# Retention and cross-attention trunk on one core: folded weights stored as hi/lo pairs, four VectorE steps given to ScalarE

## The chip, the cores and the metric

The kernel runs on one core of a Trainium2 chip. The metric is the device time of one execution in microseconds, from the runs of this one core; three runs of the kernel before took 2501.79, 2500.89 and 2510.75 us, with a median of 2501.79 us. One more execution was recorded by the hardware profiler. The core has five engines with an instruction queue each: TensorE (PE in the profile; PEld is its weight load), VectorE (DVE), ScalarE (ACT), GpSimd (POOL) and SyncE (SP), which here only issues DMAs. ACT and POOL issue some DMAs too, in line with their other instructions.

## The reference, cut to what matters

One layer of a decoder trunk over 2048 tokens of width 1024, in fp32:

```python
h = rmsnorm(x, mix_norm_g)
q, k, v, g, u = split(h @ w_in)                       # four retention heads of 128, and 512 pooling channels
y_ret  = silu(g) * head_rmsnorm(retention(rope(q), rope(k) * 128**-0.5, v), ret_gn_g)
y_pool = pool_mixer(u, pool_w, pool_scale)            # windowed means, one 128x128 matrix per group
x = x + concat([y_ret, y_pool]) @ w_out
# cross-attention into 256 memory tokens, four heads of 256
q = rmsnorm(x, xa_norm_g) @ xa_wq;  k, v = split(rmsnorm(mem, mem_norm_g) @ xa_wkv)
x = x + softmax(q @ k.T / 16) @ v @ xa_wo
x = x + conv_glu_ffn(rmsnorm(x, ffn_norm_g), ...)     # d_ff 2816, causal depthwise conv of width 3
return rmsnorm(x, final_norm_g)

def rope(t):      # t1, t2: the two halves of a head
    return concat([t1 * cos - t2 * sin, t2 * cos + t1 * sin])
```

## The kernel before, in words

Everything is held transposed, channels on the 128 partitions and tokens along the row. Matrix products keep fp32 accuracy with operands split in two: `split` (L230) lets ScalarE round a tile to the high part (`hi`, type fp32r) and VectorE subtract it from the source (`lo`), and `passes` (L239) multiplies hi by hi, hi by lo and lo by hi, three matmuls (L241, L242, L243) into one PSUM tile. Such a hi/lo couple is called a pair.

The tokens are worked in two blocks b = 0 and 1 of 1024 (`T`), each in two halves s of 512 (`SUB`). For a block come in order: values, four heads (gate, q and k, one `unit` each), four pooling groups, the output projection w_out (eight units n), the cross-attention (16 chunks of 128 tokens by two heads) and its output product (eight units with the weights VWd). Behind both blocks stands the FFN, done with sums of tiles in seven products in place of eight (`run`, L1324); the sums of its weights (`weight_sums`, L903) are made earlier by DMAs that SP and POOL issue between the units.

`folded_weights` (L360) does the products of weights alone, between the heads of block 0: the memory's keys with xa_wq into Md (L473), its values with xa_wo into VWd (L491), the pooling matrices with w_out into WPd (L512). A result is evacuated from PSUM by ScalarE into a tile of the arena `TT` (ten slots, called T in the profile), and `keep` (L431) sends it to DRAM from ScalarE's DMA queue as one fp32 tile. When it is used, in block 0 and again in block 1, it is loaded by SP into R (five slots of 1024), and split anew: by `pairs` (L255) into Q (three slots of a pair each) for VWd and WPd, and by `load_m` (L830) for Md, whose 16 tiles a pass go into the second half of G (first head pair; only its first two into Q) and into Z (second head pair). G's second half holds the inputs of w_out (`mix`) until w_out has read them.

A `unit` (L285) is 48 matmuls: two weight halves h by two token halves s by four contraction tiles by three passes. Five PSUM banks (`mm`) serve the units, three more (`aux`) the rest. `rope_evac` (L687) rotates q and k out of PSUM: one product with cos, two of 64 partitions with the crossed halves and sin, one add, all on VectorE. `retention` (L717) works a head as two halves of four chunks, as a generator that is advanced between the quarters of later units: scores, states, values, mixed. In `values` the four chunks' outputs are scaled by a factor per token (L772), in one VectorE instruction. In `attention` (L822) each chunk takes its maximum (L871), the exponentials with their sums on ScalarE (L875), the reciprocal (L877), a scaling of both heads' halves on VectorE (L880), and later the transposes and the split of `turn` (L847).

The order on each engine is made when the program is built: the code is recorded in program order, a scheduler with a model of the times reorders it, and each engine then runs its list strictly in that order. SP's list has all its loads and the copies for the weight sums; a DMA there that waits for its slot holds up those behind it. `tc.issue_after(fetched[0].ins)` (L911) places the copies for a weight sum behind the latest load. POOL's list has the adding DMAs of the weight sums and, between them, the 16-column copies of the pooling groups (L630, L631).

Of the kernel before, what the change touches and what calls it, by code (L numbers as in the profile page):

```python
# [8 lines left out]
F32 = mybir.dt.float32  # L9
# [6 lines left out]
P = 128  # L16
# [103 lines left out]
def trunk(ctx, tc, xT, memT, pos, w_qkgu, w_v, wkv, wqT, wo, wout_r, wout_p, poolT, w_up, w_dn, vecs, consts, outT):  # L120
# [164 lines left out]
    def unit(raw, rhs, evac, order=range(4)):  # L285


        hs = pairs(raw)
# [71 lines left out]
    def folded_weights():  # L360
# [74 lines left out]
        def tiles4(d, nh, k):  # L435
            return d[4 * nh : 4 * nh + 4, :, k, :].rearrange("n p c -> p n c")
# [23 lines left out]
        for h in range(HEADS):  # L460
            dp = [row_pairs(wqT[(2 * h + dt) * P : (2 * h + dt + 1) * P, :]) for dt in range(2)]
            for k2 in range(KT // 2):
# [6 lines left out]
                t = TT.take()  # L469
                for j in range(2):  # L470
                    k = 2 * k2 + j
                    act.activation(t.f[:, j * NMEM : (j + 1) * NMEM], ps[:, j * NMEM : (j + 1) * NMEM], AF.Identity, scale=xag[:, k : k + 1])
                keep(Md[h // 2, 2 * k2 : 2 * k2 + 2, :, (h % 2) * NMEM : (h % 2 + 1) * NMEM].rearrange("k p m -> p k m"), t, 2)  # L473
# [6 lines left out]
        for h in range(HEADS):  # L480
            dp = [row_pairs(wo[(2 * h + dt) * P : (2 * h + dt + 1) * P, :]) for dt in range(2)]
            for mt in range(2):
                for nh in range(2):
# [5 lines left out]
                    t = TT.take()  # L489
                    act.activation(t.f[:, :SUB], ps, AF.Identity, scale=rn[:, mt : mt + 1])  # L490
                    keep(tiles4(VWd, nh, 2 * h + mt), t, 4)  # L491
# [12 lines left out]
        for g in range(4):  # L504
            u = row_pairs(wout_p[g])
            for nh in range(2):
                ps = mmps()
                lh = [pw.r[:, i * SUB + g * P : i * SUB + (g + 1) * P] for i in range(2)]
                passes(ps, lh, [u.r[:, i * T + nh * SUB : i * T + (nh + 1) * SUB] for i in range(2)], True, True)
                t = TT.take()  # L510
                act.activation(t.f[:, :SUB], ps, AF.Copy)
                keep(tiles4(WPd, nh, g), t, 4)  # L512
# [170 lines left out]
    def head_inputs(h, rb, cs, fill):  # L683
# [3 lines left out]
        def rope_evac(i):  # L687
            def evac(s, ps):
# [28 lines left out]
    def retention(b, h, qkg, v, out):  # L717
# [10 lines left out]
        class Half:  # L728
# [30 lines left out]
            def values(self):  # L759
# [12 lines left out]
                tt(dve, four(self.kn.f[:, :SUB]), four(y), bcast(rr, P), ALU.mult)  # L772
# [49 lines left out]
    def attention(sums, beside, pace):  # L822
# [7 lines left out]
        def load_m(hp):  # L830

            out = mw[hp]
            for kp in range(KT // 2):
                raw = new_raw()
                fetched[0] = sp.dma_start(raw.rearrange("p (k n) -> p k n", k=2), Md[hp, 2 * kp : 2 * kp + 2].rearrange("k p n -> p k n"))
                if hp == 0 and kp == 0:

                    out += [(pr[:, 0], pr[:, 1]) for pr in pairs(raw)]
                    yield
                    continue  # L840
                for i in range(2):
                    u = third[2 * hp].r[:, (2 * kp + i) * T : (2 * kp + i + 1) * T]
                    split(raw[:, i * SUB : (i + 1) * SUB], u[:, :SUB], u[:, SUB:])
# [16 lines left out]
        for i in range(2 * KT):  # L860
# [638 lines left out]
    for b in range(NB):  # L1499
# [68 lines left out]
        for n in range(KT):  # L1568
# [7 lines left out]
            unit(load_tile(VWd[n]), rhs, add_residual(b, n, xs, acc=acc[n]))  # L1576
# [150 lines left out]
```

## Time and profile before

| | |
|---|---|
| median of three runs | 2501.79 us |
| the profiled execution: its time, its span | 2506.72 us, 2504.9 us |
| PE busy | 2442.7 us, 98% of the span |
| DVE busy | 1666.9 us, 67% |
| ACT busy | 1216.1 us, 49% |
| POOL busy | 652.4 us, 26% |
| moved by DMA | 474.28 MB, mean 189 GB/s |

The span is what the profiler saw of the program on the core; the execution's own time is a little longer. Times inside the profile count from the span's start. In a view by windows each row is a stretch of time with the busy time of each engine in it and, in parentheses, the number of its instructions, then the clock that was granted to TensorE (1.00 is full), the share of time in which the DMA engines were busy, and GB/s. In a list of groups a row has the line, the engine, the operation, the tiles written and read, the shapes, the count, then busy us and mean ns of one, and behind the bar the idle time of the engine just before them with what ended it. By the trace, block 0's folded weights and heads run from about 135 to 340 us, its w_out from about 384 us, its attention from 474.6 us; block 1 follows from about 680 us, and the FFN takes the second half.

### The profile page before, as it was taken

To read this page: it belongs to the slowest core of one execution; us is meant where nothing else is said; L and a number is where in the kernel's file an instruction comes from. 1 tells how busy PE (TensorE), PEld (TensorE's weight loads), DVE (VectorE), ACT (ScalarE), POOL (GpSimd) and SP (SyncE) were. 2 spreads that over 40 slices of the span, in tenths; PEclk is the share of its full clock that TensorE was granted. 3 is DMA by queue.
4 is the path that set the end of the run, shared out by engine and by line. 5 is a ranking of instruction groups with operands and counts; after the bars stand their busy time and mean duration, and the time that the engine had idled before them with its cause. 6 is when DMAs were issued, how large, how long until landed. Compare 5 with 4: busy or idle time off the path is not lost.

```text
span 2504.9 us, 33172 instructions
## 1 busy us (share of the span) xinstructions
PE 2442.7 (98%) x11390; PEld 2037.7 (81%) x11390; DVE 1666.9 (67%) x2574; ACT 1216.1 (49%) x2163; POOL 652.4 (26%) x579
## 2 busy tenths in 40 slices
PE   6999999999999999999999999999999999999997
PEld 6888887788788888888887888878888887888885
DVE  8646566564635675574678776886677586867875
ACT  6333423343321223434654555665555576666663
POOL 1010122100121120030237352553335154222322
PEclk9999999999999999999999999999999999999998
DMA  8363888715766764366567564755556468768951
GB/s 318 89 168 110 244 191 233 234 40 181 227 152 145 159 158 149 111 221 220 167 205 270 166 203 153 236 192 165 160 160 213 136 220 287 250 185 280 346 164 68
DMA packets 257177, 474.28 MB, mean 189 GB/s; under 512 B 26864, under 2 KB 56176, under 8 KB 257008
## 3 DMA queue, kind: packets, MB, share of 16 engines
q1 hardware_dynamic: 212336, 408.18, 49.0%
q0 software_dynamic: 19584, 34.61, 8.9%
q10 hardware_dynamic: 25088, 29.37, 3.4%
q8 instruction: 89, 1.46, 0.2%
q14 instruction: 80, 0.66, 0.1%
HBM read 370.87 MB, written 170.39 MB: 216 GB/s over the span
## 4 chain that ended last, share of the span: by engine, by line
PE 78%; DMA 8%; DVE 6%; issue 3%; POOL 2%; ACT 2%; SPq 0%; POOLq 0%; ACTq 0%; DVEq 0%
PE mm L241 25%; PE mm L242 24%; PE mm L243 24%; POOL T L216 1%; DVE Z L216 1%; DMA T<-Xd 1%; DVE Z L225 1%; DVE G L216 1%; DMA T<-xT 1%; DVE Q L216 1%; DVE T L216 1%; DMA T<-Gd 1%; POOL Z L216 1%; PE aux L749 1%; DMA R<-VWd 0%
## 5 line engine op out<-in xcount | busy, mean ns | idle before, releaser
L241 PE MATMUL mm<-G,Q 128*128 128x512 f32 (+1 forms) x1888 | 728.1, 386 | 21.8 <-ACT Q L233 11.1
L243 PE MATMUL mm<-G,Q 128*128 128x512 f32 (+1 forms) x1888 | 725.9, 385 | 4.4 <-DVE Q L216 4.2
L242 PE MATMUL mm<-G,Q 128*128 128x512 f32 (+1 forms) x1888 | 725.7, 385 | 0.7 <-DVE G L216 0.7
L241 PE MATMUL mm<-G 128*128 128x512 f32 (+1 forms) x1380 | 532.1, 387 | 10.0 <-DVE Z L216 6.3
L242 PE MATMUL mm<-G 128*128 128x512 f32 (+1 forms) x1380 | 531.7, 386 | 0.0
L243 PE MATMUL mm<-G 128*128 128x512 f32 (+1 forms) x1380 | 531.1, 385 | 0.0
L241 PEld LDWEIGHTS mm<-G,Q 128*128 128x128 f32 x1888 | 357.8, 190 | 91.1 <-ACT Q L233 11.8
L243 PEld LDWEIGHTS mm<-G,Q 128*128 128x128 f32 x1888 | 357.7, 190 | 74.3 <-DVE Q L216 5.9
L242 PEld LDWEIGHTS mm<-G,Q 128*128 128x128 f32 x1888 | 358.0, 190 | 69.4 <-DVE G L216 1.6
L225 DVE SCALAR_TENSOR_TENSOR Z<-Z,vecs 128x1024 f32<-128x1024 f32 x176 | 276.3, 1572 | 153.5 <-ACT Z L1069 145.3
L241 PEld LDWEIGHTS mm<-G 128*128 128x128 f32 x1380 | 260.4, 189 | 64.5 <-DVE Z L216 8.0
L243 PEld LDWEIGHTS mm<-G 128*128 128x128 f32 x1380 | 260.2, 189 | 51.8
L242 PEld LDWEIGHTS mm<-G 128*128 128x128 f32 x1380 | 260.1, 188 | 51.5
L1006 ACT ACTIVATE G<-R 128x512 fp32r<-128x512 f32 (+1 forms) x272 | 166.5, 615 | 197.8 <-PE mm L242 178.6
L216 DVE TENSOR_TENSOR Z<-Z,mm 128x512 f32<-128x512 f32 x284 | 192.8, 679 | 78.2 <-PE mm L243 78.0
L216 DVE TENSOR_TENSOR Q<-R,Q 128x512 fp32r<-128x512 f32 x199 | 148.6, 748 | 143.4 <-ACT Q L233 138.9
L216 POOL TENSOR_TENSOR G<-R,G 128x512 fp32r<-128x512 f32 (+1 forms) x100 | 141.9, 1420 | 376.2 <-ACT G L1006 290.9
L233 ACT ACTIVATE Q<-R 128x512 fp32r<-128x512 f32 x150 | 93.8, 627 | 234.8 <-PE mm L242 187.3
L1006 ACT ACTIVATE Q<-R 128x512 fp32r<-128x512 f32 (+1 forms) x204 | 125.0, 613 | 90.9 <-PE mm L242 73.5
L216 DVE TENSOR_TENSOR G<-R,G 128x512 fp32r<-128x512 f32 (+1 forms) x168 | 131.5, 794 | 46.7 <-ACT G L233 38.0
L216 DVE TENSOR_TENSOR G<-T,G 128x512 fp32r<-128x512 f32 (+1 forms) x168 | 125.4, 758 | 53.9 <-ACT G L955 40.7
L940 ACT ACTIVATE aux<-R 128x512 f32<-128x512 f32 (+1 forms) x184 | 105.8, 576 | 95.8 <-DVE Q L216 52.9
(222 smaller groups left out, 2911.4 us busy)
## 6 DMA issues: line engine op xcount, KB each, us to landing
R<-Ud SPq DMA_DIRECT2D x176, 256.0 KB, 2.7
T<-Gd SPq DMA_DIRECT2D x168, 256.0 KB, 4.1
R<-w_up SPq DMA_DIRECT2D x132, 256.0 KB, 3.1
Gd<-Z SPq DMA_DIRECT2D x110, 256.0 KB, 2.4
Ud<-w_up SPq DMA_DIRECT2D x88, 256.0 KB, 5.9
R<-w_qkgu SPq DMA_DIRECT2D x32, 512.0 KB, 4.4
R<-Dd SPq DMA_DIRECT2D x64, 256.0 KB, 4.0
Gd<-T SPq DMA_DIRECT2D x56, 256.0 KB, 3.1
```

What stands on the lines that cost most here:

```text
L216: return eng.tensor_tensor(out=out, in0=a, in1=b, op=op)
L225: dve.scalar_tensor_tensor(out=out, in0=a, scalar=s, in1=b, op0=op0, op1=op1)
L233: act.activation(hi, src, AF.Copy)
L241: pe.matmul(ps, lh, rh, start=start, stop=False, skip_group_check=more)
L242: pe.matmul(ps, lh, rl, start=False, stop=False, skip_group_check=more)
L243: pe.matmul(ps, ll, rh, start=False, stop=stop, skip_group_check=more)
L749: pe.matmul(col(self.kv, c), col(self.kn.f, c), self.ch(v, c, h * T), start=True, stop=True)
L940: act.activation(t, x, AF.Copy)
L1006: act.activation(p2[:, 0, :w], self.raw[i].f[:, :w], AF.Copy)
```

## The change

Four things are changed, all in one edit.

1. The folded weights are stored in DRAM as pairs. `keep` now takes the PSUM tile itself and two T slots, splits it on the spot (ScalarE the hi, VectorE the lo, both out of PSUM, with the scale applied in both), and sends two DMAs from ScalarE's queue. Md, VWd and WPd are twice as large.
2. The loads bring pairs. VWd and WPd go straight into the slots of Q with `load_pair`, and Md straight into G or Z, with no split and without R. In w_out the other half of the unit's weights (`wout_r`) is still loaded to R and split.
3. Rotary's two crossed halves are copied out of PSUM by ScalarE (64 partitions each); VectorE then multiplies the whole copied tile by sin in one instruction.
4. Softmax's division is a ScalarE activation with a scale per token in place of a VectorE instruction, and the scaling of the retention's output is four ScalarE activations, one per chunk, in place of one VectorE instruction.

```diff
-    Md = drp.tile([2, KT, P, SUB], F32, tag="Md", name="Md")
-    VWd = drp.tile([KT, P, KT, P], F32, tag="VWd", name="VWd")
+    Md = drp.tile([2, KT, P, 2, SUB], F32, tag="Md", name="Md")
+    VWd = drp.tile([KT, 2, P, 2, 4, P], F32, tag="VWd", name="VWd")
...
-    WPd = drp.tile([KT, P, 4, P], F32, tag="WPd", name="WPd")
+    WPd = drp.tile([KT, P, 2, 4, P], F32, tag="WPd", name="WPd")
...
+    def load_pair(src):
+        pr = new_pair()
+        fetched[0] = sp.dma_start(pr.bitcast(F32), src)
+        return pr
...
-        hs = pairs(raw)
+        hs = raw if isinstance(raw, list) else pairs(raw)
...
-        def keep(dst, t, n):
-            act.dma_start(dst, t.f[:, :SUB].rearrange("p (n c) -> p n c", n=n))
-            t.free()
+        def keep(dsts, ps, n, g=None):
+            two = [TT.take() for _ in range(2)]
+            hi, lo = (t.f[:, :SUB].bitcast(F32R) for t in two)
+            w = SUB // n
+            for j in range(n if isinstance(g, list) else 1):
+                at = slice(j * w, (j + 1) * w) if isinstance(g, list) else slice(0, SUB)
+                split(ps[:, at], hi[:, at], lo[:, at], g[j] if isinstance(g, list) else g)
+            for t, dst in zip(two, dsts):
+                act.dma_start(dst, t.f[:, :SUB].rearrange("p (n c) -> p n c", n=n))
+                t.free()
...
-                    t = TT.take()
-                    act.activation(t.f[:, :SUB], ps, AF.Identity, scale=rn[:, mt : mt + 1])
-                    keep(tiles4(VWd, nh, 2 * h + mt), t, 4)
+                    to = VWd[4 * nh : 4 * nh + 4, h // 2, :, :, 2 * (h % 2) + mt]
+                    keep([to[:, :, i].rearrange("n p c -> p n c") for i in range(2)], ps, 4, rn[:, mt : mt + 1])
...
+                act.activation(w[0:64], ps[64:128], AF.Copy)
+                act.activation(w[64:128], ps[0:64], AF.Copy)
                 tt(dve, d, ps, c, ALU.mult)
-                tt(dve, w[0:64], ps[64:128], sn[0:64], ALU.mult)
-                tt(dve, w[64:128], ps[0:64], sn[64:128], ALU.mult)
+                tt(dve, w, w, sn, ALU.mult)
...
-                tt(dve, four(self.kn.f[:, :SUB]), four(y), bcast(rr, P), ALU.mult)
+                for c in range(4):
+                    act.activation(col(self.kn.f, c), col(y, c), AF.Identity, scale=rr[:, c : c + 1])
...
-                raw = new_raw()
-                fetched[0] = sp.dma_start(raw.rearrange("p (k n) -> p k n", k=2), Md[hp, 2 * kp : 2 * kp + 2].rearrange("k p n -> p k n"))
-                if hp == 0 and kp == 0:
-
-                    out += [(pr[:, 0], pr[:, 1]) for pr in pairs(raw)]
-                    yield
-                    continue
-                for i in range(2):
-                    u = third[2 * hp].r[:, (2 * kp + i) * T : (2 * kp + i + 1) * T]
-                    split(raw[:, i * SUB : (i + 1) * SUB], u[:, :SUB], u[:, SUB:])
+                for k in (2 * kp, 2 * kp + 1):
+                    if hp == 0 and kp == 0:
+                        pr = load_pair(Md[hp, k])
+                        out.append((pr[:, 0], pr[:, 1]))
+                        continue
+                    u = third[2 * hp].r[:, k * T : (k + 1) * T]
+                    fetched[0] = sp.dma_start(u.bitcast(F32), Md[hp, k].rearrange("p i n -> p (i n)"))
                     out.append((u[:, :SUB], u[:, SUB:]))
...
-                ts(dve, ej, ej, sm[:, j : j + 1], ALU.mult)
+                act.activation(ej, ej, AF.Identity, scale=sm[:, j : j + 1])
...
-            fetched[0] = sp.dma_start(raw[:, SUB:], WPd[n].rearrange("p k c -> p (k c)"))
+            pr = new_pair()
+            split(raw[:, :SUB], pr[:, 0], pr[:, 1])
+            raw = [pr, load_pair(WPd[n].rearrange("p i k c -> p i (k c)"))]
...
-            unit(load_tile(VWd[n]), rhs, add_residual(b, n, xs, acc=acc[n]))
+            unit([load_pair(VWd[n, h].rearrange("p i k c -> p i (k c)")) for h in range(2)], rhs, add_residual(b, n, xs, acc=acc[n]))
```

More of the change, by code (lines that the diff above doesn't have):

```diff
@@ L429, in row_pairs @@
             return u
-        def keep(dst, t, n):
-            act.dma_start(dst, t.f[:, :SUB].rearrange("p (n c) -> p n c", n=n))
-            t.free()
-        def tiles4(d, nh, k):
-            return d[4 * nh : 4 * nh + 4, :, k, :].rearrange("n p c -> p n c")
+        def keep(dsts, ps, n, g=None):
[8 more added lines that the diff above has]
+                t.free()
         kk = B.take(4)
@@ L468, in folded_weights @@
                         passes(ps[:, j * NMEM : (j + 1) * NMEM], w, (kp4[:, 2 * h + dt, 0], kp4[:, 2 * h + dt, 1]), dt == 0, dt == 1)
-                t = TT.take()
[L470 to L473, printed above, removed]
+                to = Md[h // 2, 2 * k2 : 2 * k2 + 2, :, :, (h % 2) * NMEM : (h % 2 + 1) * NMEM]
+                keep([to[:, :, i].rearrange("k p m -> p k m") for i in range(2)], ps, 2, [xag[:, 2 * k2 + j : 2 * k2 + j + 1] for j in range(2)])
             for u in dp:
@@ L488, in folded_weights @@
                         passes(ps, lh, w, dt == 0, dt == 1)
-                    t = TT.take()
-                    act.activation(t.f[:, :SUB], ps, AF.Identity, scale=rn[:, mt : mt + 1])
-                    keep(tiles4(VWd, nh, 2 * h + mt), t, 4)
+                    to = VWd[4 * nh : 4 * nh + 4, h // 2, :, :, 2 * (h % 2) + mt]
+                    keep([to[:, :, i].rearrange("n p c -> p n c") for i in range(2)], ps, 4, rn[:, mt : mt + 1])
             for u in dp:
@@ L509, in folded_weights @@
                 passes(ps, lh, [u.r[:, i * T + nh * SUB : i * T + (nh + 1) * SUB] for i in range(2)], True, True)
-                t = TT.take()
-                act.activation(t.f[:, :SUB], ps, AF.Copy)
-                keep(tiles4(WPd, nh, g), t, 4)
+                to = WPd[4 * nh : 4 * nh + 4, :, :, g]
+                keep([to[:, :, i].rearrange("n p c -> p n c") for i in range(2)], ps, 4)
             u.free()
```

## The prediction

> **What bounds the kernel now.** I began with the page's totals.
>
> ```profile
> span 2504.9 us, 33172 instructions
> PE 2442.7 (98%) x11390; PEld 2037.7 (81%) x11390; DVE 1666.9 (67%) x2574; ACT 1216.1 (49%) x2163; POOL 652.4 (26%) x579
> ```
>
> TensorE is busy 98% of the span, so 2504.9 − 2442.7 = 62 us of idle and some slow clock is all that work on other engines can give back, and only in the stages that the change touches. The windows say where it lies. In this view a row is a stretch of time, the busy us of each engine with its instructions, the clock granted to TensorE, DMA share and GB/s.
>
> ```profile
> 250.00:275.00 25.00, 24.48 (x111) 20.05 (x110) 16.65 (x36) 10.30 (x17) 2.44 (x3) 1.00 0.83 240
> 275.00:300.00 25.00, 24.67 (x132) 20.87 (x131) 9.45 (x17) 12.02 (x20) 2.44 (x3) 1.00 0.87 251
> 300.00:325.00 25.00, 25.00 (x127) 21.11 (x127) 18.02 (x48) 8.67 (x27) 4.96 (x6) 1.00 0.81 182
> 325.00:350.00 25.00, 25.00 (x135) 21.49 (x135) 15.18 (x33) 8.63 (x21) 4.25 (x8) 1.00 0.82 224
> 350.00:375.00 25.00, 24.70 (x126) 20.72 (x125) 17.48 (x46) 5.14 (x15) 7.44 (x14) 1.00 0.86 184
> 375.00:400.00 25.00, 21.24 (x91) 16.70 (x90) 15.96 (x28) 4.28 (x7) 9.12 (x14) 1.00 0.81 183
> 400.00:425.00 25.00, 25.00 (x112) 20.68 (x111) 17.42 (x29) 10.98 (x19) 4.38 (x6) 1.00 1.01 297
> 425.00:450.00 25.00, 25.00 (x112) 20.71 (x111) 11.21 (x17) 7.78 (x13) 0.81 (x1) 1.00 0.55 178
> 450.00:475.00 25.00, 25.00 (x112) 20.71 (x111) 16.07 (x26) 12.11 (x22) 2.47 (x3) 1.00 0.70 217
> 475.00:500.00 25.00, 21.62 (x103) 17.77 (x102) 11.17 (x30) 7.54 (x14) 6.59 (x8) 1.00 1.07 300
> 500.00:525.00 25.00, 24.04 (x110) 19.92 (x111) 23.36 (x58) 10.99 (x30) 0.81 (x1) 0.93 0.16 30
> 525.00:550.00 25.00, 25.00 (x119) 20.62 (x118) 13.39 (x34) 16.47 (x35) 0.00 (x0) 1.00 0.22 74
> 550.00:575.00 25.00, 25.00 (x119) 20.63 (x118) 12.69 (x29) 8.90 (x24) 0.00 (x0) 1.00 0.00 1
> 650.00:675.00 25.00, 23.91 (x110) 19.91 (x110) 17.43 (x28) 13.03 (x23) 2.15 (x3) 0.93 0.56 187
> 675.00:700.00 25.00, 23.31 (x109) 19.17 (x109) 13.93 (x44) 3.92 (x7) 7.42 (x12) 1.00 1.07 310
> ```
>
> A full window of projections holds 112 matmuls in 25.00 us, 0.223 us each. Three places of block 0 fall short: 375 to 400 (21.24 of 25), 475 to 525, and 650 to 700. The chain of waits names what ended each.
>
> ```profile
> 264.02 11.29 DMA VWd<-T
> 373.64 7.30 DMA Ud<-w_up
> 481.77 12.46 DMA R<-VWd
> 494.33 0.64 ACT Q L233
> 670.07 6.08 DMA R<-w_v
> ```
>
> At 494 ScalarE stood in front of the split of the first VWd tile, whose load was 12.46 us under way, with the softmax of the first attention chunks behind it in its list; then the transposes stood still. At 670 block 1's first w_v was late. At 374 POOL's halo copies stood behind an accumulating DMA that waited for a w_up load. TensorE's own waits agree in size:
>
> ```profile
> PE mm L241 <- ACT Q L233: 11.1, 4, 9.0
> PE aux L850 <- DVE T L220: 4.5, 2, 4.3
> PE aux L339 <- DVE G L216: 1.7, 1, 1.7
> ```
>
> The 9.0 us are the start of the kernel and stay; 4.3 us are the transposes after softmax, 1.7 us the first norm of block 1.
>
> **The change part by part.** I sum against the profiled execution, 2506.72 us, which is 4.93 above the median of the runs, 2501.79; the same sum is then taken from the median.
>
> *Engine time.* The removed and the nearest rows for the added:
>
> ```profile
> L216 DVE TENSOR_TENSOR T<-mm,Z 64x512 f32<-64x512 f32 x64 | 44.0, 688 | 1.1
> L220 DVE TENSOR_SCALAR T<-T,sm 128x256 f32<-128x256 f32 x64 | 25.5, 441 | 1.0
> L216 DVE TENSOR_TENSOR T<-aux,sm 128x512 f32<-128x512 f32 x16 | 11.1, 691 | 1.0
> L216 DVE TENSOR_TENSOR Q<-R,Q 128x512 fp32r<-128x512 f32 x199 | 148.6, 748 | 143.4 <-ACT Q L233 138.9 <-ACT Q L1006 3.9
> L216 DVE TENSOR_TENSOR T<-mm,T 128x512 f32<-128x512 f32 x32 | 21.9, 688 | 23.5 <-PE mm L243 19.2 <-POOL phalo L631 4.3
> L233 ACT ACTIVATE Q<-R 128x512 fp32r<-128x512 f32 x150 | 93.8, 627 | 234.8 <-PE mm L242 187.3 <-DMA R<-w_qkgu 13.2 <-DMA R<-VWd 11.2
> L472 ACT ACTIVATE T<-mm,vecs 128x256 f32<-128x256 f32 x32 | 13.3, 473 | 6.0 <-PE mm L243 3.7 <-PE aux L777 2.2
> L490 ACT ACTIVATE T<-mm,rnm 128x512 f32<-128x512 f32 x16 | 10.9, 687 | 11.4 <-DMA VWd<-T 6.6 <-PE mm L243 2.2 <-ACT T L490 1.4
> L511 ACT ACTIVATE T<-mm 128x512 f32<-128x512 f32 x8 | 4.7, 596 | 3.3 <-PE mm L243 1.4 <-PE aux L777 1.2 <-DMA WPd<-T 0.7
> L768 ACT ACTIVATE T<-aux 128x128 f32<-128x128 f32 x64 | 16.8, 276 | 26.0 <-PE aux L764 26.0
> ```
>
> Rotary: 64 half products (44.0 us) go from VectorE, 32 whole ones come (32 × 688 ns = 22.0); ScalarE gets 64 half copies at about 596 ns (38.1). Softmax: 64 × 441 ns (25.5 us) become 64 × about 473 ns (30.3) on ScalarE. Retention: 16 × 691 ns (11.1) become 64 × about 276 ns (17.7). Pairs: 80 splits after loads go (32 + 16 tiles of VWd and WPd, 32 of Md), 80 × 748 ns = 59.8 on VectorE and 80 × 627 = 50.2 on ScalarE; the 40 evacuations stay on ScalarE and VectorE gets 40 lows of at most 688 ns (27.5). Net VectorE −44.0 + 22.0 − 25.5 − 11.1 − 59.8 + 27.5 = −91 us, ScalarE +38.1 + 30.3 + 17.7 − 50.2 = +36 us. At 67% and 49% both lie beside TensorE; by themselves these sums move nothing. Their ends as a price run from below nothing (VectorE's waits shorten) to the rival on ScalarE below. In one rotary the chain is 3 × 688 = 2.07 us before the add, and 2 × 596 + 688 = 1.88 after, if the two engines take turns at the bank: nothing. Cover is the five PSUM banks of the next units; without it each of 32 would cost up to 0.6 us more if ScalarE comes late.
>
> *The three stalls.* (1) 475 to 525 held 213 matmuls where the next 50 us hold 238; 25 of them at 50/238 us are 5.3 us. In the changed order no split stands before softmax on ScalarE, and the load of the VWd pair goes past no engine that softmax needs. It goes: **−5.3**, ends −5.3 and 0. Next late is the M tiles (below). (2) 650 to 700: idle 1.09 + 1.69 = 2.8 us and 0.07 × 25 = 1.75 us of slow clock, 4.5 together. With Md, VWd and WPd no longer passing through the five R slots, SP's list has w_v and w_qkgu of block 1 far earlier. The splits and the norm's spread remain: **−3**, ends −4.5 and 0. (3) 375 to 400: 3.8 us idle. Four of POOL's halo copies now stand ahead of the adding DMAs, and the w_up loads are earlier on SP; the last halo still stands behind one: **−2**, ends −3.8 and 0.
>
> *The folds.* A pair holds two of the ten T slots; by the listing, norm tables and gates hold four during the folds, so three results are in flight in place of six. VWd's come in two bursts of eight banks, each of 6 matmuls, 1.34 us. The row of one of them in the chain, the DMA group and the landings of the tile's DMAs:
>
> ```profile
> VWd<-T ACTq DMA_DIRECT2D x16, 256.0 KB, 5.7
> DMA to landing us min/median/max: 2.3/5.7/17.2
> ```
>
> With hi and lo at 0.69 each, the first result has left its slots at 1.34 + 1.38 + L for a landing of L. Then the fourth bank's evacuation starts, done at 4.1 + L; the unit behind the burst wants this bank at 8 × 1.34 = 10.7. So L up to 6.6 costs nothing. The median of 5.7 is below, the 11.29 row far above. With twice the bytes I take 8.1, nearer to the median than to the worst: 1.5 us for each burst, **+3**, ends 0 and 25 (rival 1). The DMAs are 10.5 MB more written and 21 MB more read; 12.6 MB of these fall in 250 to 500 us, 42 us at the 300 GB/s of the row of 475, and the DMA shares of these rows leave 1.75 × 25 = 44 us free. It just fits, which is why I don't put the folds at nothing.
>
> *Md straight into G.*
>
> ```profile
> R<-Md SPq DMA_DIRECT2D x16, 512.0 KB, 3.8
> ```
>
> The first pass's tiles now wait for G slots that w_out's last units free. By the listing six 512 KB loads start about 5.5 us ahead of w_out's end; at 300 GB/s one takes 1.75 us, so they land up to 10.5 − 5.5 = 5 us behind it and the last is wanted at some 13: **+1** for both blocks, ends 0 and 8.4 (rival 2). Z's tiles are loaded ahead of w_out. On SP's queue a tile that waits holds up the loads behind it, but these are of w_out's end or later.
>
> *Retention's output* gets four activations (1.1 us) for one of 0.69 in a chain two quarters long: **+0.5**: nearer to nothing, because the quarter of a unit behind it (12 × 0.223 = 2.7 us) covers it mostly. Ends: +6.6 = 16 × (4 × 0.276 − 0.691) with no cover, and −0.5, since VectorE's list ahead of the next split is shorter.
>
> Sum: −5.3 − 3 − 2 + 3 + 1 + 0.5 = **−5.8 us**: 2500.9 for the profiled execution, 2496.0 for the median. From 1400 us on the listing has the same FFN order on both; it stays.
>
> After the 4.3 us wait the clock fell to 0.93 of a window, 1.75 us; 375 to 400, with 3.8 us idle in pieces, kept 1.00. The Trainium skill, "TensorE: Matmul & The Clock Gate", Part 1, has a free-running window of about 3.4 us of idleness behind which the clock is halved; both rows agree with that, and by it the first stall's removal would return its slow clock too, which the count of matmuls holds already.
>
> **The rivals.** Rival 1, T slots starve (slower than before): if VWd's landings in the bursts are like the 11.29 row, the unit waits 11.29 − 6.6 = 4.7 us, and 1.7 of slow clock as at 500, twice: 12.8. −5.8 − 3 + 12.8 = +4.0, 2505.8. It decides from L = 9.3 (2 × (2.7 + 1.7) = 8.8). With L = 17.2: 2 × (10.6 + 1.7) = 24.6, 2517.6. For it: the share of 0.83 to 0.87 already there. Against: in the row of 490 ScalarE waited 6.6 us for such a slot and TensorE idled only 0.5 + 0.3 us in both windows.
>
> Rival 2, M tiles gate attention: at half the rate the last lands at 21 − 5.5 = 15.5 against 13; 2.5 and 1.7 of clock, for two passes 8.4: 2496.0 − 1 + 8.4 = 2503.4. For it: shares of 1.07 at 475; against: that traffic has by then less behind it, since VWd and the weights come earlier.
>
> Rival 3, ScalarE is the wrong engine: 6.6 us for retention and 64 × (0.473 − 0.441) = 2.0 for softmax all on the path: 2504.6. At 7.5 to 16.5 us busy in attention's windows of 25 it has room. The Trainium skill, "ScalarE: Activation LUTs", Rules for kernel authors, says multiplies belong on VectorE; no row here compares both at one shape, and the nearest (473 to 441, 276 × 4 to 691) agree.
>
> Rival 4, the stalls only move to the next late transfer: 2501.8. Rival 5, all three go whole and nothing new comes: −5.3 − 4.5 − 3.8 = −13.6, 2488.2.
>
> **How the numbers follow.** Half a per cent (12.5 us) is what a measurement here tells from no change: faster is below 2489.3, slower above 2514.3. Forecast 0.43, rival 1 0.18 (0.07 of it beyond 2514), rival 2 0.11 (0.05 of it together with rival 1, and beyond 2514), rival 3 0.06, rival 4 0.09, rival 5 0.13. Faster: rival 5, 0.13, and 0.01 of the forecast's edge; slower: 0.07 + 0.05 = 0.12; the rest, 0.74, between. The range leaves out 0.07 below (half of rival 5, whose 2488.2 has 3 us of scatter under it: 2485) and 0.12 above: 2513. Signs are mixed; the forecast's own range is 2491 to 2501.
>
> **What would show it.** Right: 475 to 525 holds 235 matmuls or more; no wait of L850 over 1 us; the 1.7 us of L339 gone; ScalarE 36 us busier and VectorE 91 less; windows 250 to 300 as full as now. Wrong: waits of TensorE on ScalarE's fold evacuations with a VWd DMA in the chain (rival 1); waits for DMA into G behind w_out (rival 2); a wait on the retention's scaling or a softmax activation (rival 3).

## The result, and the profile after

The changed kernel took 2573.49 us (median; 2570.43 to 2576.17) against 2500.89 us for the kernel before in the same measurement: a ratio of 1.0283, with a 95% interval of 1.026 to 1.0306. It is 72.6 us slower where 5.8 us less was forecast, and outside the range of 2485 to 2513. The profiled execution's span grew by 67.0 us, from 2504.9 to 2571.9 us. The page of the changed kernel begins:

```profile
span 2571.9 us, 33194 instructions
PE 2467.2 (96%) x11390; PEld 2052.0 (80%) x11390; DVE 1590.1 (62%) x2438; ACT 1253.5 (49%) x2273; POOL 656.5 (26%) x579
```

VectorE lost 76.8 us of work (91 forecast) and ScalarE gained 37.4 (36 forecast), so the arithmetic of the engines came out close to what was written. None of it shortened the run. The matmuls are the same 11390, yet TensorE is busy 24.5 us longer: its mean granted clock fell from 0.992 to 0.982. Of the 67.0 us, 42.5 are more idle time and 24.5 this slower clock. The two traces have the same number of matmuls, so the time at which the matmul of the same number starts, before and after, shows where the 67 us arose (worked out from the starts in the traces; inside a stage the order differs a little, at these places it lines up):

| matmul | place | before, us | after − before, us |
|---|---|---|---|
| 900 | folds of Md under way | 175.3 | +1.4 |
| 1860 | folds and heads of block 0 done | 355.6 | +26.6 |
| 2040 | first units of w_out, block 0 | 398.0 | +21.5 |
| 2460 | attention of block 0 under way | 491.5 | +64.4 |
| 2520 | behind the softmax stall of before | 510.1 | +58.6 |
| 4560 | heads of block 1 done | 932.4 | +57.0 |
| 5520 | output product of block 1 | 1143.0 | +67.6 |
| 11389 | last | 2494.9 | +67.0 |

So 25 us went in the folds (the products of weights alone, and the heads worked between them), 43 in w_out of block 0 and the start of its attention, some 10 in block 1's w_out and output product, and the FFN is the same. The drops between (−5.1 by matmul 2040, −5.8 by 2520, −2.9 around matmul 3300) are the three stalls that the forecast removed; a new stall of 1.2 us stands just ahead of the last. The windows of the changed kernel over the folds and w_out, in the columns of those shown before:

```profile
200.00:250.00 50.00, 45.44 (x249) 39.93 (x249) 29.55 (x64) 24.03 (x60) 0.00 (x0) 0.93 0.49 158
250.00:300.00 50.00, 40.85 (x191) 33.26 (x190) 30.37 (x68) 23.97 (x50) 3.26 (x4) 0.93 0.72 195
300.00:350.00 50.00, 47.44 (x235) 39.89 (x234) 26.90 (x66) 22.19 (x54) 6.54 (x8) 0.97 0.93 247
350.00:400.00 50.00, 48.89 (x250) 40.65 (x250) 34.82 (x81) 18.16 (x48) 4.18 (x9) 1.00 0.41 124
400.00:450.00 50.00, 42.94 (x180) 34.41 (x179) 25.72 (x44) 9.53 (x16) 19.70 (x26) 0.93 1.06 310
450.00:500.00 50.00, 37.82 (x144) 29.52 (x143) 9.27 (x15) 5.87 (x10) 10.73 (x13) 0.90 1.08 305
500.00:550.00 50.00, 42.16 (x163) 33.47 (x162) 19.73 (x41) 11.21 (x19) 10.81 (x13) 0.86 1.05 311
```

From 400 to 550 us the DMA engines are full (1.05 to 1.08), ScalarE is busy 5.9 to 11.2 of 50 us and VectorE 9.3 to 25.7: TensorE waits for data. Just before, at 350 to 400, the DMA share was 0.41. In a list of waits a row has who waited for what, then the us in all, how many times, and the longest. TensorE's list, beside a wait that had 11.1 us before (the first row), names two kinds that the list of before does not have:

```profile
PE mm L241 <- ACT Q L233: 18.4, 9, 9.3
PE mm L241 <- DMA Q<-WPd: 18.1, 5, 6.6
PE mm L241 <- DVE T L225: 10.6, 3, 4.5
PE mm L241 <- DMA Q<-VWd: 3.9, 2, 2.8
```

They are the loads of the WPd and VWd pairs (18.1 and 3.9 us) and VectorE's evacuation of the folded results (10.6 us). The chain of waits shows what stood behind both:

```profile
267.08 8.79 DMA VWd<-T
417.01 12.26 DMA Ud<-w_up
429.29 14.31 DMA Ud<-w_up
484.68 15.34 DMA Ud<-w_up
512.27 11.85 DMA Q<-WPd
```

and VectorE's list shows the first of them as a wait for a T slot:

```profile
270.14 0.23 DVE L220 TENSOR_SCALAR sm<-sm,consts 128x4 f32<-128x4 f32 x1
275.98 0.75 DVE L225 SCALAR_TENSOR_TENSOR T<-mm,rnm,T 128x512 fp32r<-128x512 f32 x1 [5.61 <-DMA VWd<-T]
276.65 0.74 DVE L225 SCALAR_TENSOR_TENSOR T<-aux,vecs,T 128x512 f32<-128x512 f32 x1
```

For 5.61 us VectorE stood in front of one lo whose slot was still being sent to DRAM. The instruction behind it (gate times the retention's output, at 276.65) and the next lo (277.49) then came late too, and TensorE with them. ScalarE had stood in the same way just before, 5.13 us in front of a hi.

### The profile page after: what moved, and what is told of

Its sections match the earlier page's. It is cut to its first block, busy times and chain, and to the rows that moved or that the text cites. A ratio compares the mean times of both kernels' runs of the same rounds, so it can differ in the third digit from the quotient of the medians.

```text
span 2571.9 us, 33194 instructions
## 1 busy us (share of the span) xinstructions
PE 2467.2 (96%) x11390; PEld 2052.0 (80%) x11390; DVE 1590.1 (62%) x2438; ACT 1253.5 (49%) x2273; POOL 656.5 (26%) x579
## 4 chain that ended last, share of the span: by engine, by line
PE 74%; DMA 14%; DVE 4%; issue 3%; POOL 2%; ACT 2%; SPq 1%; ACTq 0%; POOLq 0%; DVEq 0%
PE mm L241 24%; PE mm L242 23%; PE mm L243 23%; DMA Ud<-w_up 3%; DMA T<-Gd 1%; POOL T L216 1%; DMA Q<-WPd 1%; DVE G L216 1%; DMA VWd<-T 1%; DMA T<-Xd 1%; DVE Z L216 1%; DMA T<-xT 1%; DMA Dd<-w_dn 1%; DVE Z L225 1%; DMA Q<-VWd 1%
## 5 line engine op out<-in xcount | busy, mean ns | idle before, releaser
L241 PE MATMUL mm<-G 128*128 128x512 f32 (+1 forms) x1380 | 535.9, 389 | 21.2 <-DVE T L225 10.6
L243 PEld LDWEIGHTS mm<-G,Q 128*128 128x128 f32 x1888 | 359.5, 191 | 76.8 <-DVE Q L216 7.3
L216 DVE TENSOR_TENSOR Q<-R,Q 128x512 fp32r<-128x512 f32 x147 | 111.9, 763 | 101.0 <-ACT Q L233 87.4
L216 DVE TENSOR_TENSOR G<-T,G 128x512 fp32r<-128x512 f32 (+1 forms) x171 | 130.7, 774 | 60.0 <-ACT G L959 41.7
L216 DVE TENSOR_TENSOR T<-T 128x512 f32<-128x512 f32 (+4 forms) x153 | 107.5, 711 | 78.9 <-ACT T L360 62.0
L216 DVE TENSOR_TENSOR G<-R,G 128x512 fp32r<-128x512 f32 (+1 forms) x156 | 125.6, 818 | 29.1 <-ACT G L233 19.3
```

What stands on the lines that cost most here:

```text
L216: return eng.tensor_tensor(out=out, in0=a, in1=b, op=op)
L241: pe.matmul(ps, lh, rh, start=start, stop=False, skip_group_check=more)
L243: pe.matmul(ps, ll, rh, start=False, stop=stop, skip_group_check=more)
```

## The experiments

In each the time is compared with the kernel before on the same chip. The changed kernel was measured once, so a gain or loss against it in total time compares two chips; where the intervals of the two ratios overlap, this is said. The kernels' own places against before, at the matmuls of the table above, are given where they carry the reading.

**1. ScalarE's three steps alone, and 2. the pairs alone.**

```diff
# run 1, on the kernel before; run 2 has all the rest of the change and none of this
-tt(dve, w[0:64], ps[64:128], sn[0:64], ALU.mult)
-tt(dve, w[64:128], ps[0:64], sn[64:128], ALU.mult)
+act.activation(w[0:64], ps[64:128], AF.Copy)
+act.activation(w[64:128], ps[0:64], AF.Copy)
+tt(dve, w, w, sn, ALU.mult)
...
-tt(dve, four(self.kn.f[:, :SUB]), four(y), bcast(rr, P), ALU.mult)
+for c in range(4):
+    act.activation(col(self.kn.f, c), col(y, c), AF.Identity, scale=rr[:, c : c + 1])
...
-ts(dve, ej, ej, sm[:, j : j + 1], ALU.mult)
+act.activation(ej, ej, AF.Identity, scale=sm[:, j : j + 1])
```

> The kernel before with the rotary copies, the softmax scaling and the retention scaling on ScalarE; folded weights as before. Theory A (the pairs alone made the 71 us: their two T slots for each result, their landing in the three slots of Q, and the weight-sum copies that SP then issues late and in a heap): ratio to before 0.997 to 1.003. Theory B (ScalarE's new steps stand in front of what TensorE waits for): ratio 1.01 or more.

Measured 2510.97 us, ratio 1.0019 (1.0008 to 1.003): a small loss, 2 to 7.5 us.

> The changed kernel with rotary, softmax and retention as before; only the folded weights are pairs. Theory A: ratio to before 1.025 to 1.031, the whole loss. Theory B: at most 1.015.

Measured 2573.44 us, ratio 1.0267 (1.0245 to 1.0289); +23.1 us at matmul 1860, +53.9 at 2520, +69.4 at 5520. The pairs alone make the loss, and it lies where the changed kernel has it. The theory that ScalarE's steps stand in front falls as the cause of it.

**3. Twice the T slots, the same bytes.**

```diff
-t = TT.take()
-act.activation(t.f[:, :SUB], ps, AF.Identity, scale=rn[:, mt : mt + 1])
+two = [TT.take() for _ in range(2)]
+for j, t in enumerate(two):
+    act.activation(t.f[:, :NMEM], ps[:, j * NMEM : (j + 1) * NMEM], AF.Identity, scale=g[j])
+    act.dma_start(dst[:, j * n // 2 : (j + 1) * n // 2], ...)
```

> The kernel before, but each folded result is evacuated as two halves into two T slots and sent by two DMAs of half the size: twice the slots, the same bytes, loads as before. If the slots alone make the 26 us that the changed kernel lost in the folds (matmuls 900 to 1860): 15 to 30 us over before, 1.006 to 1.012. If it is the doubled bytes and the later landings: under 8 us, at most 1.003.

Measured 2531.44 us, ratio 1.0101 (1.0078 to 1.0124), the number expected, but from another place: only 5.6 us had gone by matmul 1860. Eleven more came by 2040, where TensorE waited 7.1 us at the transposes of a retention's output for VectorE, and 6 between 2520 and 4560. In the folds ScalarE waited for slots four times in VWd's bursts, 2.0 to 4.6 us, and VectorE once in Md's, 3.3 us. So slots without VectorE's wait cost the folds little. Why the edit loses twice as much again behind them isn't shown; a shifted order is a guess.

**4. The copies behind the loads into R.** The copies for the weight sums are told to be issued behind the latest load; here the loads of pairs don't count as such.

```diff
-fetched[0] = sp.dma_start(pr.bitcast(F32), src)     # load_pair, and Md's loads alike
+sp.dma_start(pr.bitcast(F32), src)
-sp.dma_start(raw[:, :SUB], wout_r[n]...)
+fetched[0] = sp.dma_start(raw[:, :SUB], wout_r[n]...)
```

> The changed kernel, but the copies for the weight sums are placed behind the latest load into R (wout_r among them) and no longer behind the loads of pairs into Q, G and Z. If the heap of copies behind the late pair loads makes the 43 us that w_out of block 0 lost: 20 to 45 us under the changed kernel, ratio to before 1.010 to 1.020, and the DMA share of 400 to 550 us falls from 1.06 to under 0.95. If the landing in three Q slots alone makes it: within 10 us of the changed kernel, 1.024 or more.

Measured 2565.96 us, ratio 1.0241 (1.0211 to 1.0271): by the medians 7.5 us under the changed kernel (the intervals overlap), where 20 to 45 were expected. More copies ran before w_out, and 6 us more were lost there (+32.5 at 1860 in place of 26.6); w_out lost 22 us in place of 37 between 2040 and 2520. The DMA share of 400 to 550 us fell to 0.93 in the mean, as was expected if the copies make the loss, but most of the loss stayed. Moving the copies moves a part of it.

**5, 6, 7. One table of pairs at a time.** Each is run 2 with the other two tables taken back to one fp32 tile; for WPd alone the edit against the kernel before is

```diff
-WPd = drp.tile([KT, P, 4, P], F32, tag="WPd", name="WPd")
+WPd = drp.tile([KT, P, 2, 4, P], F32, tag="WPd", name="WPd")
...
-fetched[0] = sp.dma_start(raw[:, SUB:], WPd[n].rearrange("p k c -> p (k c)"))
+pr = new_pair()
+split(raw[:, :SUB], pr[:, 0], pr[:, 1])
+raw = [pr, load_pair(WPd[n].rearrange("p i k c -> p i (k c)"))]
```

> Only WPd is stored and loaded as pairs; Md, VWd and ScalarE's steps as before. If the landing in the three slots of Q (a load can't start before the pair before it was read by TensorE) makes the loss of w_out by itself: 20 to 45 us over before (ratio 1.008 to 1.018), with waits of TensorE on the WPd loads in both blocks. If it is the heap of other traffic in that stage (Md's tiles loaded early, doubled bytes): under 8 us, at most 1.003.

> Only VWd is stored and loaded as pairs. T slots: the folds lose 10 to 20 us between 250 and 350 us and the output product of block 1 about 4, the softmax stall at 495 goes (-5): ratio 1.003 to 1.008. If the folds only lose with all three together: 0.996 to 1.001.

> Only Md is stored and loaded as pairs. If its early loads into Z hold SP's list up and push the copies and loads of w_out together: 15 to 45 us over before, nearly all between 380 and 520 us (ratio 1.006 to 1.018). If its part is only the T slots of its folds: 5 to 10 us by 260 us, nothing behind (1.002 to 1.004).

Measured: WPd 2522.09 us, 1.0071 (1.0054 to 1.0087); VWd 2529.56 us, 1.0102 (1.0085 to 1.012); Md 2523.44 us, 1.0077 (1.006 to 1.0094). Over the 2504.86 us of before these are 17.2, 24.7 and 18.6 us, in sum 60.5, near the 67 of all three. None of the three fell cleanly on one side of what was expected. Each loses some 7 to 10 us by 1860 (VWd 10.5, Md 8.1, WPd 7.2), and each loses again in w_out, attention or behind. VWd lost more than was expected for it, and more than half of it outside the folds. With Md alone the DMA share was already 1.07 at 400 to 450 us, and TensorE was busy 41.34 of those 50 us.

**8. Md's loads behind WPd's.**

```diff
+behind_wp = fetched[0].ins
+with tc.issue_after(behind_wp):
     fetched[0] = sp.dma_start(u.bitcast(F32), Md[hp, k]...)
```

> The changed kernel with all its loads of Md on SP behind the last load of WPd. If the early Z loads make the loss of w_out in block 0: 20 to 45 us under the changed kernel (ratio to before 1.010 to 1.020). If it is the landing in Q: within 10 us of the changed kernel (1.024 or more), and attention may wait for M besides.

Measured 2590.51 us, ratio 1.0343 (1.0327 to 1.0358): slower still. The early Z loads are not the cause: w_out without them was only 8 us better by matmul 2280, and TensorE then waited 22.0 us, at the norm in front of attention, for VectorE's sum of squares.

**9. The results in G's slots.**

```diff
-two = [TT.take() for _ in range(2)]
-hi, lo = (t.f[:, :SUB].bitcast(F32R) for t in two)
+one = B.take()
+hi, lo = one.r[:, :SUB], one.r[:, SUB:]
```

> The changed kernel, but a folded result's hi and lo go to one free slot of G's second half (as wide as both) in place of two T slots; the same bytes and DMAs. If the folds lose their 26 us to T slots (VectorE's lo waits for a slot, and all that stands behind it on VectorE waits too): 18 to 28 us under the changed kernel, ratio to before 1.017 to 1.021, and no stall over 2 us of TensorE on VectorE's fold evacuations between 200 and 330 us. If the doubled bytes make it: within 8 us of the changed kernel.

Measured 2567.78 us, ratio 1.0258 (1.0236 to 1.0281), 5.7 us under the changed kernel (the intervals overlap), where 18 to 28 were expected. At matmul 1440 the loss is 0.9 us where the changed kernel had some 20: the waits of TensorE on VectorE's fold evacuations are gone. Then one wait of 9.7 us takes their place, on ScalarE. The rows are from this kernel's waits of TensorE and from ScalarE's timeline:

```profile
PE mm L241 <- ACT G L233: 12.3, 3, 9.7
```

```profile
280.32 8.03 ACTq L445 DMA_DIRECT2D VWd<-G  x6
288.41 0.63 ACT L233 ACTIVATE G<-R 128x512 fp32r<-128x512 f32 x1 [8.38 <-DMA VWd<-G]
```

ScalarE now waits 8.38 us to write the next row's hi into a slot that a result is still leaving. The slots were the cause of TensorE's waits on VectorE; another arena has the same wait at another place. At 1860 the loss is 14.5 us in place of 26.6, a gain of 12; by 2520 9 of it are left (+49.6 for 58.6), at the end 6.

**10. WPd's pairs land in Z.** Eight slots, empty then, in place of Q's three.

```diff
+land = new_z(F32R).take(KT)
-raw = [pr, load_pair(WPd[n]...)]
+u = land.r[:, n * T : (n + 1) * T]
+fetched[0] = sp.dma_start(u.bitcast(F32), WPd[n]...)
+raw = [pr, u.rearrange("p (i n) -> p i n", i=2)]
```

> The changed kernel, but WPd's eight pairs land in the eight slots of Z, empty at that time, in place of Q; Md's second half is loaded behind them. If landing in three Q slots makes the 43 us of w_out in block 0: 20 to 40 us under the changed kernel, ratio to before 1.012 to 1.020, no waits of TensorE on WPd loads. If the heap of traffic makes it: within 12 us of the changed kernel, 1.023 or more.

Measured 2549.6 us, ratio 1.0186 (1.0167 to 1.0206), 24 us under the changed kernel. Between 2040 and 2520 it loses 13.6 us where the changed kernel loses 37.1. What is left there is one wait of 16.1 us; the rows are of its waits and of its chain:

```profile
PE mm L241 <- DVE T L216: 21.0, 3, 16.1
```

```profile
428.81 13.12 DMA Ud<-w_up
442.00 8.48 DMA T<-xT
```

No wait for WPd is left, though five of the eight loads still took 9.9 to 15.1 us to land: they were issued earlier. The next load behind the copies on SP, the residual's x, is late in its place.

**11. No adding jobs in w_out of block 0.** The jobs that make the weight sums, SP's copies and POOL's adding DMAs, rest in this stage.

```diff
+if b == 0:
+    under, stopped = [iter(())], under      # ahead of w_out
...
+if b == 0:
+    under = stopped                         # behind attention
```

> The changed kernel, but the adding jobs of the weight sums rest during w_out and attention of block 0 and go on with its output product. If the traffic of their copies, bunched in this stage, makes the 43 us: at matmul 2460 the loss against before is 35 us or more smaller than in the changed kernel's 64, the DMA share of 400 to 500 us falls below 0.9, and waits on WPd loads are under 3 us in all. If the landing in Q makes it: at most 10 us smaller. What the later copies cost behind is a separate term.

Measured 2578.56 us, ratio 1.0301 (1.0281 to 1.0321). The total is no better (the intervals overlap), but the place is telling. Windows of w_out and attention of block 0, then of w_out of block 1, to which the jobs are now pushed:

```profile
400.00:450.00 50.00, 50.00 (x223) 41.37 (x222) 33.71 (x57) 15.09 (x26) 11.99 (x11) 1.00 0.72 220
450.00:500.00 50.00, 50.00 (x230) 41.66 (x229) 17.65 (x29) 10.51 (x18) 0.58 (x1) 1.00 0.69 237
500.00:550.00 50.00, 50.00 (x235) 41.24 (x234) 29.54 (x73) 28.98 (x68) 0.00 (x0) 1.00 0.18 59
...
950.00:1000.00 50.00, 26.75 (x96) 20.06 (x96) 7.47 (x11) 4.34 (x8) 11.77 (x16) 0.81 1.07 323
1000.00:1050.00 50.00, 40.26 (x153) 31.31 (x154) 17.07 (x26) 11.44 (x19) 17.58 (x23) 0.85 1.09 283
```

Block 0 has no idle at all, with the same pairs landing in the same three slots, and loses nothing between 2040 and 2520 (from +16.4 to +10.6: the softmax stall's gain). Block 1 then loses 52 us between 4560 and 5160; TensorE waited there 22.7 us for ScalarE's splits of weights loaded through R and 8.9 us for WPd. The landing times of the WPd tile's loads from 400 to 530 us (min, median, max us), eight of the changed kernel and seven of this one:

```profile
DMA to landing us min/median/max: 7.6/12.9/17.8
```

```profile
DMA to landing us min/median/max: 3.2/5.2/6.9
```

A pair takes 12.9 us to land with the copies and 5.2 without.

**12, 14, 15. ScalarE's steps one by one,** each alone on the kernel before: the third, the first and the second part of run 1's diff.

> The kernel before with only the softmax scaling on ScalarE. The first experiment lost 5.9 us less in attention of block 0 than before and gave 4.8 back between 290 and 350 us, where rotary and retention run. If the gain is softmax's: ratio 0.9970 to 0.9985. If the order shifted by chance: 0.999 to 1.002.

> The kernel before with only rotary's crossed halves copied by ScalarE. All three steps together measured 1.0019 and softmax alone 0.9988, so rotary and retention should add to 1.003. If rotary's copies make it: 1.002 to 1.004; if retention's four activations make it: 0.999 to 1.001.

> The kernel before with only the retention's scaling as four activations. Prediction's term was +0.5 us with an end of 6.6. If the four activations stand on the chain: 1.002 to 1.003 (5 to 7 us); if they are covered: 0.999 to 1.001.

Measured: softmax 2500.25 us, ratio 0.9988 (0.9977 to 0.9999); rotary 2509.28 us, 1.0013 (1.0002 to 1.0024); retention 2504.35 us, 0.9996 (0.9987 to 1.0005). By the medians softmax's scaling gains some 3 us, rotary's copies cost about as much (0.5 to 6 us by the interval), and retention's four activations cost nothing that shows. Softmax and rotary each fell between their two forecasts. The three don't add to the 1.0019 of all together.

**13. The kernel before, its jobs resting in the same way.** This is the control for run 11, with the diff of run 11 on the kernel before: the same push of copies into block 1, without pairs.

> The kernel before with the adding jobs resting in w_out and attention of block 0, as in the eleventh run: they are then done in block 1 and meet its w_out. If it is the pairs' traffic together with the copies that overfills a w_out stage: block 1's w_out and attention (matmuls 4560 to 5040) lose under 15 us here where they lost 53 with pairs, ratio to before at most 1.006. If the copies alone overfill any w_out into which they are pushed: 35 us or more there, ratio 1.012 or more.

Measured 2495.3 us, ratio 0.9961 (0.9949 to 0.9974): 10 us faster than before.

```profile
950.00:1000.00 50.00, 50.00 (x223) 41.38 (x222) 26.75 (x42) 18.49 (x32) 3.68 (x5) 1.00 0.65 195
1000.00:1050.00 50.00, 50.00 (x239) 41.57 (x238) 28.66 (x73) 20.92 (x49) 16.34 (x20) 1.00 1.08 291
```

Block 1 stays full with the copies in it, even at a DMA share of 1.08, and the three stalls of block 0 are gone (−0.8 at 2040, −6.7 at 2520, −11.4 at 4560). It is not the whole of a control: by the issues in the traces 51 transfers for the weight sums fell between matmuls 4560 and 5040, against 94 in run 11, where the jobs had come later all along.

**16. Both gains together,** run 13 with softmax's scaling on ScalarE (the third part of run 1's diff).

> The kernel before with the adding jobs resting in w_out and attention of block 0 and softmax's scaling on ScalarE. The two measured 0.9961 and 0.9988. If they gain at different places: 0.994 to 0.996. If both only remove the same stall of attention of block 0: 0.996 to 0.997, no more than the rest alone.

Measured 2494.83 us, ratio 0.9969 (0.9958 to 0.9981): no more than the resting jobs alone, as was expected if both only remove the same stall. That is in line with the traces: between 2460 and 2520 each of runs 13 and 16 gains 5.8 us on before.

**17. The bytes alone.** The kernel before with 8.4 MB more of loads on SP in w_out of block 0.

```diff
+land = new_z(F32).take(KT) if b == 0 else None
+for i in range(2):
+    sp.dma_start(land.f[:, n * T : (n + 1) * T], VWd[(n + i) % KT]...)
```

> The kernel before with sixteen more loads of 512 KB on SP's queue in w_out of block 0, into the empty slots of Z, read by nobody: 8.4 MB beside the same copies, about what pairs add there (WPd 2.1 MB, Md 4.2 MB, next weights earlier 2 to 3 MB). If bytes that meet the copies make the loss in w_out: 20 to 45 us between matmuls 2040 and 2520, ratio 1.008 to 1.018. If the deferred copies or the landing in Q make it: under 10 us, at most 1.004.

Measured 2500.12 us, ratio 0.9984 (0.997 to 0.9997). The DMA share rose to 0.99 and 0.97 between 350 and 450 us and TensorE lost nothing there. Three of the eight loads of WPd took 10.9 to 12.7 us to land, and TensorE waited for none: they had been issued long before. More bytes beside the copies don't make the loss by themselves, and neither do slow landings of loads that start early.

## Why the prediction was wrong

*The stalls (−5.3, −3, −2): they went, and a little more than forecast; for the first the reason isn't shown.* They gave 5.8, 2.9 and 5.1 us, against the −10.3 of the sum. The forecast's reason for the first was that no split of VWd stands in front of softmax any more. Run 6, with VWd's pairs alone, agrees with it: the 5.8 us are gone. But they are gone as well in runs 5, 7, 15 and 17, which load VWd through R and split it as before. In runs 15 and 17 ScalarE waited 7.0 and 6.5 us for the first VWd tile in place of 11.2, and that was enough. So this part was in some measure luck: a shift of 3 to 6 us in the landing of one load removes the stall, whatever the edit aims at.

*Engine time: near.* Softmax's scaling took 502 ns for 473, rotary's copies 596 and 591 for 596, retention's activations 367 for 276; the rows are the changed kernel's groups.

```profile
L884 ACT ACTIVATE T<-T,sm 128x256 f32<-128x256 f32 x64 | 28.9, 502 | 11.5 <-DVE sm L881 11.5
L702 ACT ACTIVATE T<-mm 64x512 f32<-64x512 f32 x32 | 19.1, 596 | 23.3 <-PE mm L243 10.2 <-DVE G L216 4.9 <-PE aux L784 4.8
L703 ACT ACTIVATE T<-mm 64x512 f32<-64x512 f32 x32 | 18.9, 591 | 0.4
L779 ACT ACTIVATE T<-aux,sm 128x128 f32<-128x128 f32 x64 | 18.2, 367 | 20.5 <-DVE sm L220 20.5
```

The term of +0.5 for the retention stands within its measurement (run 15), and rival 3 falls in both its parts: retention's price didn't come, and softmax went the other way. Rotary's copies, which the sum had at nothing, cost 0.5 to 6 us (run 14). The Trainium skill, "ScalarE: Activation LUTs", Rules for kernel authors, gives such multiplies to VectorE; the durations agree with it (502 ns against 441 on VectorE), the time of run 12 did not follow them (ratio 0.9988).

*The folds (+3, ends 0 and 25): the step that failed is the price, and the model under it.* It asked when the PSUM bank of the fourth result was wanted by the unit behind the burst, as if only that bank's evacuation waited. The runs showed 25.2 us. The lo is an instruction of VectorE's list, and while it waits for a slot everything behind it waits, work for TensorE among it; so Md's folds, which the step did not price at all, lost as well (TensorE waited 4.5 us from 214.8 us on), and the threshold of 6.6 us meant nothing. Run 9 took the T slots away and with them these waits; run 3 held two slots for each result without a lo on VectorE and lost 5.6 us in the folds. How the 25.2 us divide between VectorE's waits, ScalarE's and the slower clock behind them (0.93 from 200 to 300 us) is not measured. The Trainium skill, "PSUM — Partial Sum Buffer", section Engine vs sequencer instructions, says that ScalarE's and VectorE's queues are strictly in order; the row at 275.98 agrees. The prediction's point against rival 1, that ScalarE's wait of 6.6 us in the kernel before cost TensorE only 0.8, was true of that wait and did not carry over to VectorE. Rival 1 named the slots; that its highest price, 24.6 us, was about right is luck, since it priced VWd's two bursts alone, while runs 5, 6 and 7 lost 7.2, 10.5 and 8.1 us by matmul 1860 with WPd's, VWd's and Md's pairs.

*The loads of WPd and VWd: the step that failed outright.* "The load of the VWd pair goes past no engine that softmax needs" was right, and no term was written for how late a pair's load can start and how long it then takes to land; that term, put at nothing, measured 43 us in w_out of block 0. In the kernel before WPd went into R, and its first load was issued at 334 us, 50 us before w_out began. A slot of Q becomes free only when TensorE has read the pair in it, so with three slots a load can start two pairs ahead, 48 matmuls or 10.7 us. That covers a landing of 5.2 us (run 11, with the same slots and no stall) and not one of 12.9.

In the changed kernel the loads started later still. The rows are of its SP and ScalarE timelines:

```profile
401.40 10.06 SPq L917 DMA_DIRECT2D Ud<-w_up  x6
411.65 0.44 SPq L267 DMA_DIRECT2D Q<-WPd  x1
```

```profile
490.27 0.33 ACTq L821 DMA_DIRECT2D Xd<-T  x1
490.65 0.63 ACT L360 ACTIVATE T<-T 128x512 f32<-128x512 f32 x1 [15.52 <-DMA Ud<-w_up]
```

The load at 411.65 was issued 0.06 us after the landing (411.59) of the transfer issued eight places earlier, and so were four more of the eight WPd loads of this stage, counting SP's and ScalarE's transfers together; two came close behind another transfer that had waited in this way, and only the last was issued as TensorE freed a slot. In run 11 six of the eight were issued as TensorE freed a slot. In no trace of this case are more than eight transfers of these two lists under way at once. Between matmuls 2040 and 2520, 55 of 83 issues on these lists in the changed kernel found seven transfers still under way, 3 of 57 in run 11 and 16 of 66 in the kernel before. So when the copies land slowly, all that stands behind them on SP is late, and ScalarE too, which stood 15.52 us in front of its own store of the residual (Xd). In line with this, TensorE waited from 400 to 545 us not only for WPd (15.4 us) but also for ScalarE's splits of the half that still comes through R (6.7 us). Whether the chip or the building of the program sets the bound of eight isn't shown, and no run changed it.

The copies for the weight sums came late as well: counted from the issues, 47 transfers for them between matmuls 1140 and 2040 against 62 before, then 65 between 2040 and the end of the stage against 34. Take away the copies (run 11) and the 43 us are gone; issue the WPd loads earlier (run 10) and 24 are gone; add only bytes to loads that start early (run 17) and nothing is lost. Together these show that the loss of w_out needs both late starts and slow landings. How much of the late start is the three slots and how much the full lists was not separated. The sum's "it just fits", 42 us of traffic into 44 us of free share, was an average over 250 us and hid that the traffic would come in 150.

*Md into G (+1) and rival 2.* Attention waited 1.5 us for one M tile; the term holds. *Block 1* had no term and lost 10 us; TensorE waited there 2.7 us for WPd and 3.9 for VWd, so the same missing step is likely, and no run was made on it.

What stays open: why the copies came late. Two things stand before them on SP, loads of wout_r that wait for R and loads of Md that wait for Z; run 4 changed what the copies are placed behind and run 8 moved Md, and by the medians run 4 brought the total down by 7.5 us and run 8 raised it. Nor were runs 9 and 10 joined, or the copies put on a list of their own.

## What to carry to other kernels

A format that saves work on an engine pays only if the tiles it needs have places to wait. Before a load is sent straight to where it is read, count how many can be under way there, and compare with how far ahead the old buffer let them start. Count as well how many transfers an engine's list can have under way, since a load behind slow copies starts only when one of them has landed. Before an evacuation takes two slots, look at which engine will stand still in its in-order list when there is none. And when a stage already has optional transfers in it, try resting those first: that alone gave 10 us here.

## What the runs showed of the hardware

Landing times grew when the DMA engines were full: at a DMA share of 1.05 to 1.08 and 305 to 311 GB/s a 512 KB load of WPd took 12.9 us to land in the changed kernel, at 0.69 to 0.72 and 220 to 237 GB/s 5.2 us in run 11. A share of 1.08 in run 13 cost TensorE nothing, so a full DMA window by itself says nothing of a stall. In no trace here were more than eight transfers of SP and ScalarE together under way at once.

Idle time of TensorE cost clock besides: with the same 11390 matmuls its busy time rose from 2442.7 to 2467.2 us as the mean granted clock fell from 0.992 to 0.982. It was 1.00 in run 11's windows without idle time from 400 to 550 us, and 0.86 to 0.93 in those of the changed kernel.

Single steps did not add up: three steps of ScalarE measured 0.9988, 0.9996 and 1.0013 alone and 1.0019 together, and an edit that only added reads (run 17) came out 0.2% faster. In run 17's trace the stall of before at the softmax is gone without anything that aims at it.
